# Products of constants ahead of the transposes and the decays of the first pair of heads

## The chip, the cores and the metric

The kernel runs on one core of one Trainium2 chip. The metric is the device time in microseconds (us) of one execution; less is better. A core has five engines that each work through a list of instructions of their own, in order: TensorE (PE in the profile: matrix products, and transposes as products), VectorE (DVE), ScalarE (ACT), GpSimd (POOL) and SyncE (SP, which only issues transfers here). They wait for one another through semaphores. Products land in PSUM, in banks of 128 x 512 fp32 numbers.

## The reference

One layer of a flow-matching backbone: 512 latent tokens and 256 context tokens of 1024 channels. Two mixers read the same modulated and normalised input: a bidirectional gated DeltaNet (GDN, 8 heads of 128) and an attention with low-rank keys and values. Their outputs are merged through sigmoid gates, and a squared-ReLU MLP follows. The part around the change is the GDN's input and the small matrices of its chunks:

```
qkv = silu(centred_conv(h @ w_qkv, conv_w))          # 5 taps over the tokens
q, k, v = split(qkv);  q, k = l2norm(q), l2norm(k)   # 8 heads x 128
g = -exp(a_log) * softplus(decay_logit + dt_bias);  beta = sigmoid(beta_logit)
# per head, direction and chunk of tokens:
decay = tril(exp(gc_i - gc_j))                       # gc: running sum of g
a_mat = strict_tril((beta k) k^T * decay)
t_mat = inverse(I + a_mat)                           # unit lower triangular
u, w = t_mat (beta v),  t_mat (beta k exp(gc))
qk = tril(q k^T * decay)
for each chunk: v_new = u - w S;  o = q_dec S + qk v_new;  S = S exp(g_last) + k_dec^T v_new
y = rms(o) * silu(z)                                 # z: a further projection of h
```

## The kernel before

**Products.** Activations and weights are fp32, split into a high and a low part of type fp32r (`hTh`, `hTl` for the latent input, `cTh`, `cTl` for the context, `wh`, `wl` for the weights). A product is made of three passes: high x high, high x low and low x high (`mm3`, lines 183 to 185 of before). `wchunk` loads a weight chunk (L176), casts it to `wh` on ScalarE (L177) and takes `wl` on VectorE (L178).

**PSUM.** The banks go by tags: `d` (two banks, projections), `t` (one, transposes of the inputs), `p` (two), `c` (two) and `e` (one, the decays and the products of k with k).

**A pair of heads.** The eight heads are worked on in four pairs. `gdn_in(pr)` takes, for each of the pair's two heads, K, then V, then Q: `project` (24 products of 128x512 into a `d` bank and, for K and V, 24 of 128x256 for the context into another), `convolve` (ScalarE copies the bank to `raw`, L467 and L469, and starts the sum of the five taps, L470; VectorE adds four taps, L472; ScalarE takes a tanh, L474; VectorE closes the silu, L475), and `transposes` (blocks of 128 tokens, four to a bank `t`, L488). What reads the transposes is ScalarE (for V: L522).

Between V and Q, `gdn_gram` makes the decays: for three groups of two blocks it sums running logarithms by products with a constant triangle `maskr` into bank `e` (L578), takes their exp on ScalarE (L584) into `QK` (or a buffer of its own), scales it (L589, L591), overwrites bank `e` by the products of k with k (`pk`, L596) and multiplies (`A`, L597, VectorE). ScalarE then copies the diagonal blocks of `A` to `Da` (L604) and sends them to memory (L607).

`gdn_prep(pr)` inverts the diagonal blocks: a recursion of 30 steps of two VectorE instructions each (L635, L636) on `pt`. Then ScalarE issues the transfers that put the result in its new places: `dB` (L640), `dC` (four, L643), the loads `D` from `dB` (L645) and `Q` from `dC` (L647). The chain over the chunks follows (`gdn_chain`, `gdn_out`).

**The order of the work.** The program is written as pair 0's inputs, pair 0's preparation, pair 1's inputs, a filling of six projections at low priority (`z_chunk`: a projection into a `d` bank, a tanh to `tz` on ScalarE, L880, and a VectorE instruction, L881, that reads the bank for the last time), pair 0's chain, and so on. A scheduler that runs when the program is built decides the order of each engine's list from priorities and from its own times; on the chip each list is fixed. So an added instruction can move others.

Of the kernel before, what the change touches and what calls it, by code (L numbers as in the profile page):

```python
# [18 lines left out]
KT = 8  # L19
# [58 lines left out]
def f32(ap):  # L78
    return ap.bitcast(F32)
# [3 lines left out]
def tile_layer(ctx, tc, I, out, stop=None, dbg=None):  # L83
# [4 lines left out]
    pe = nc.tensor  # L88

    def bc(ap, shape):  # L90
        return ap.to_broadcast(shape)
# [8 lines left out]
    def bank(tag):  # L100
        return ps.tile([P, 512], F32, tag=tag, name=tag, bufs=banks[tag])

    def v4(t):
        return t.rearrange("p (a b) -> p a b", b=128)
# [3 lines left out]
    hTh = hp.tile([P, KT, NL], F32R, name="hTh")  # L108
# [245 lines left out]
    maskr = cst.tile([P, 2, P], F32R, name="maskr")  # L354
# [66 lines left out]
    for b0, n in ((0, 4), (4, 2)):  # L421
        t = bank("t")[:, :128 * n]
# [18 lines left out]
    def project(chunk, with_ctx):  # L441
        pl = bank("d")
        pc = bank("d")[:, :NC] if with_ctx else None
        for k0 in (0, 4):
            for kt in range(k0, k0 + 4):
                mm3(pl, *chunk[kt], hTh[:, kt, :], hTl[:, kt, :], kt == 0, kt == KT - 1)
            if with_ctx:
                for kt in range(k0, k0 + 4):
                    mm3(pc, *chunk[kt], cTh[:, kt, :], cTl[:, kt, :], kt == 0, kt == KT - 1)
        return pl, pc  # L450
# [9 lines left out]
    def at(b):  # L460
        return 128 * b + (GAP if b >= 2 else 0)
# [14 lines left out]
        if pc is not None:  # L476
            pool.memset(raw[:, GAP + NC:GAP + NC + GAP], 0.0)

    def transposes(src, nb, tag):

        res = []
        b = 0
        while b < nb:
            n = min(4, nb - b)
            t = bank(tag)
            for q in range(n):
                c = at(b + q) if nb == 6 else 128 * (b + q)
                pe.transpose(t[:, 128 * q:128 * q + 128], src[:, c:c + 128], ident)  # L488
            res.append((t, b, n))
            b += n  # L490
        return res

    def gdn_in(pr):
        kT = gp.tile([P, 2, NG], F32, tag="kT", name="kT", bufs=2)
        qT = gp.tile([P, 2, NL], F32, tag="qT", name="qT", bufs=2)
        kn = gp.tile([P, 2, 6, P], F32, tag="kn", name="kn", bufs=2)
        vn = gp.tile([P, 2, 6, P], F32, tag="vn", name="vn", bufs=2)
        ssq = gp.tile([P, 2, 6], F32, tag="ssq", name="ssq", bufs=2)
        ssk = gp.tile([P, 2, 6], F32, tag="ssk", name="ssk", bufs=2)
        nk = gp.tile([P, 2, 6], F32, tag="nk", name="nk", bufs=2)  # L500
        r2 = gp.tile([P, 2, 6], F32, tag="r2", name="r2", bufs=2)
        junk = gx.tile([P, P], F32, tag="junk", name="junk")
        for h in range(2):
            hd = 2 * pr + h
            pl, pc = project(wchunk(I["w_qkv"][8 + hd]), True)
            convolve(pl, pc, 8 + hd, kT[:, h, :])
            for t, b, n in transposes(kT[:, h, :], 6, "t"):
                act.copy(kn[:, h, b:b + n, :], v4(t)[:, :n, :])
                for q in range(n):
                    act.activation(junk, kn[:, h, b + q, :], AF.Square, accum_out=ssk[:, h, b + q:b + q + 1])  # L510
            dve.tensor_scalar(ssk[:, h, :], ssk[:, h, :], EPS, None, op0=ALU.add)
            power(nk[:, h, :], ssk[:, h, :], 6, True)
            dve.reciprocal(r2[:, h, :], ssk[:, h, :])
        res = (kT, qT, kn, vn, ssq, ssk, nk, r2)
        for h in range(2):
            hd = 2 * pr + h
            vT = gx.tile([P, NG], F32, tag="vT", name="vT")
            pl, pc = project(wchunk(I["w_qkv"][16 + hd]), True)
            convolve(pl, pc, 16 + hd, vT)
            for t, b, n in transposes(vT, 6, "t"):  # L520
                for q in range(n):
                    act.activation(vn[:, h, b + q, :], t[:, 128 * q:128 * q + 128], AF.Copy,  # L522
                                   scale=nk[:, h, b + q:b + q + 1])
        gram = gdn_gram(pr, res)
        for h in range(2):
            hd = 2 * pr + h
            pl, _ = project(wchunk(I["w_qkv"][hd]), False)
            convolve(pl, None, hd, qT[:, h, :])
            for t, b, n in transposes(qT[:, h, :], 4, "t"):
                for q in range(n):  # L530
                    act.activation(junk, t[:, 128 * q:128 * q + 128], AF.Square,
                                   accum_out=ssq[:, h, b + q:b + q + 1])
        return res, gram
# [14 lines left out]
    def gdn_gram(pr, ops):  # L548
        kT, qT, kn, vn, ssq, ssk, nk, r2 = ops
# [13 lines left out]
        QK = gp.tile([P, 8, P], F32, tag="QK", name="QK", bufs=2)  # L563
        for b2 in range(3):
            pg = bank("e")
            for bb in range(2):
                b = 2 * b2 + bb
                rr = []
                for d in range(2):
                    for src in (ghi, glo):  # L570
                        t = gx.tile([P, 2, P], F32R, tag=f"rh{len(rr)}", name="rh")
                        sgn = 1 if d == 0 else -1
                        pool.affine_select(t, bc(f32(src[:, b, 8 * d + h0:8 * d + h0 + 2]).unsqueeze(2), [P, 2, P]),
                                           pattern=[[0, 2], [sgn, P]], compare_op=ALU.is_ge, fill=0.0, base=0,
                                           channel_multiplier=-sgn)
                        rr.append(t)
                for q in range(4):
                    pe.matmul(pg[:, 256 * bb:256 * bb + 256], maskr[:, q // 2, :],  # L578
                              rr[q].rearrange("p a b -> p (a b)"), start=(q == 0), stop=(q == 3))
            if b2 == 0:  # L580
                gam = gx.tile([P, 4, P], F32, tag="Bt", name="gam", bufs=2)
            else:
                gam = QK[:, 4 * b2 - 4:4 * b2, :]
            act.activation(gam, v4(pg), AF.Exp)  # L584
            Bt = gx.tile([P, 4, P], F32, tag="Bt", name="Bt", bufs=2)
            for bb in range(2):
                for h in range(2):
                    b = 2 * b2 + bb
                    act.activation(Bt[:, 2 * bb + h, :], f32(maskr[:, 1, :]), AF.Identity,  # L589
                                   scale=sA[:, b, 0, h:h + 1], bias=sA[:, b, 1, h:h + 1])  # L590
            dve.tensor_tensor(Bt, Bt, gam, ALU.mult)  # L591
            pk = bank("e")
            for bb in range(2):
                for h in range(2):
                    s = kT[:, h, at(2 * b2 + bb):at(2 * b2 + bb) + 128]
                    pe.matmul(v4(pk)[:, 2 * bb + h, :], s, s, start=True, stop=True)  # L596
            dve.tensor_tensor(A[:, 4 * b2:4 * b2 + 4, :], v4(pk), Bt, ALU.mult)  # L597
# [796 lines left out]
```

## Time and profile before

| | |
|---|---|
| three runs | 1318.79, 1320.42, 1323.58 us; median 1320.42 |
| profiled execution | 1319.97 us, of which the span of the trace is 1318.2 |
| PE / DVE / ACT / POOL busy | 95% / 65% / 49% / 20% of the span |
| mean granted clock of TensorE | 0.984 of 2.4 GHz |

The busy share is an average over stages with different limits. The clock that TensorE is granted has two levels, 1.2 and 2.4 GHz; in a view of a stretch 0.50 is the lower one all through it and 1.00 the upper one. In a timeline, the brackets at the end of a row hold the idle time of the engine ahead of the row and what ended it.

### The profile page before, as it was taken

What the parts mean: (1) busy time and instruction counts of PE and PEld (TensorE: products, weight loads), DVE (VectorE), ACT (ScalarE), POOL (GpSimd) and SP (SyncE); (2) the same over time, 40 slices, a digit from 0 to 9 for tenths busy, and PEclk for the clock granted to TensorE, in tenths of its full rate; (3) what the DMA queues carried; (4) which work ended last, traced back from release to release, by engine and by line L of the source; (5) the groups of instructions that cost most, each with busy time, mean ns of one, the idle gap of its engine ahead of it and who ended that gap; (6) DMA issues with size and microseconds to landing.
All of it is one profiled execution on the core that took longest, in us unless ns stands there. A gap on an engine that the chain in (4) does not pass through costs nothing. (4 is left out here: it accounts for less than half of the span.)

```text
span 1318.2 us, 21055 instructions
## 1 busy us (share of the span) xinstructions
PE 1249.4 (95%) x7406; PEld 1090.4 (83%) x7406; DVE 855.9 (65%) x1853; ACT 651.1 (49%) x1670; POOL 262.6 (20%) x369
## 2 busy tenths in 40 slices
PE   5899997988999899999989999999999999999998
PEld 4797876877889788889989998888997888888887
DVE  4655798777788768848678788676885333333332
ACT  4557574546753765366566676223453242242331
POOL 0022424314421431122100011232032010010110
PEclk9999998999999899999999999999999999999999
DMA  9332214440334114542111114766452232322232
GB/s 359 112 114 71 71 56 102 130 96 2 97 105 128 48 65 120 141 146 91 35 49 42 40 45 157 265 213 250 167 183 92 96 100 95 98 97 96 97 111 89
DMA packets 112168, 147.39 MB, mean 112 GB/s; under 512 B 45328, under 2 KB 54592, under 8 KB 111936
## 3 DMA queue, kind: packets, MB, share of 16 engines
q1 hardware_dynamic: 69728, 130.31, 29.8%
q10 hardware_dynamic: 42336, 15.76, 5.0%
q8 instruction: 58, 0.95, 0.3%
q14 instruction: 46, 0.38, 0.1%
HBM read 128.83 MB, written 17.20 MB: 111 GB/s over the span
## 5 line engine op out<-in xcount | busy, mean ns | idle before, releaser
L177 ACT CAST wh<-wf 128x512 fp32r<-128x512 f32 (+2 forms) x292 | 177.2, 610 | 358.5 <-PE d L184 288.4
L178 DVE TENSOR_TENSOR wl<-wf,wh 128x512 fp32r<-128x512 f32 (+2 forms) x268 | 183.4, 688 | 173.1 <-ACT wh L177 166.6
L183 PE MATMUL d<-hTh,wh 128*128 128x512 f32 x384 | 158.6, 413 | 5.8 <-DVE tz L881 3.5
L184 PE MATMUL d<-hTl,wh 128*128 128x512 f32 x384 | 155.6, 406 | 0.0
L185 PE MATMUL d<-hTh,wl 128*128 128x512 f32 x384 | 154.9, 403 | 0.0
L183 PE MATMUL d<-ah,wh 128*128 128x512 f32 x256 | 100.2, 393 | 0.0
L185 PE MATMUL d<-ah,wl 128*128 128x512 f32 x256 | 100.0, 393 | 0.0
L184 PE MATMUL d<-al,wh 128*128 128x512 f32 x256 | 99.3, 390 | 0.0
L183 PEld LDWEIGHTS d<-hTh,wh 128*128 128x128 f32 x384 | 74.7, 195 | 21.4 <-DVE tz L881 3.9
L1252 POOL TENSOR_TENSOR a<-r 128x512 f32<-128x512 f32 (+1 forms) x36 | 37.2, 1034 | 266.9 <-ACT r L1250 260.8
L185 PE MATMUL d<-h2h,wl 128*128 128x512 f32 x224 | 87.5, 390 | 1.7 <-DVE wl L178 1.7
L183 PE MATMUL d<-h2h,wh 128*128 128x512 f32 x224 | 87.3, 390 | 0.0
L184 PE MATMUL d<-h2l,wh 128*128 128x512 f32 x224 | 87.2, 389 | 0.0
L185 PEld LDWEIGHTS d<-hTh,wl 128*128 128x128 f32 x384 | 74.4, 194 | 15.3 <-issue 0.4
L184 PEld LDWEIGHTS d<-hTl,wh 128*128 128x128 f32 x384 | 74.8, 195 | 13.4
L1291 DVE SCALAR_TENSOR_TENSOR x<-d,mcol,x 128x512 f32<-128x512 f32 x32 | 24.0, 751 | 59.6 <-PE d L185 59.6
L178 POOL TENSOR_TENSOR wl<-wf,wh 128x512 fp32r<-128x512 f32 x24 | 35.4, 1476 | 130.7 <-ACT wh L177 130.7
L185 PEld LDWEIGHTS d<-ah,wl 128*128 128x128 f32 x256 | 48.1, 188 | 10.8
L184 PEld LDWEIGHTS d<-al,wh 128*128 128x128 f32 x256 | 48.1, 188 | 10.8
L183 PEld LDWEIGHTS d<-ah,wh 128*128 128x128 f32 x256 | 48.1, 188 | 9.8
L185 PEld LDWEIGHTS d<-h2h,wl 128*128 128x128 f32 x224 | 42.1, 188 | 10.9 <-DVE wl L178 2.1
L184 PEld LDWEIGHTS d<-h2l,wh 128*128 128x128 f32 x224 | 42.1, 188 | 8.8
(540 smaller groups left out, 3385.2 us busy)
## 6 DMA issues: line engine op xcount, KB each, us to landing
wf<-in_w_mi SPq DMA_DIRECT2D x64, 256.0 KB
wf<-in_w_mo SPq DMA_DIRECT2D x64, 256.0 KB
wf<-in_w_qkv SPq DMA_DIRECT2D x48, 256.0 KB
wm<-in_w_mod SPq DMA_DIRECT2D x40, 256.0 KB
wm<-in_w_mod SPq DMA_DIRECT2D x16, 512.0 KB
wf<-in_w_gate SPq DMA_DIRECT2D x32, 256.0 KB
wms<-in_w_mod SPq DMA_DIRECT2D x12, 512.0 KB
wf<-in_w_z SPq DMA_DIRECT2D x16, 256.0 KB
```

The source lines that it names most:

```text
L177: act.copy(wh, wf)
L178: eng.tensor_tensor(wl, wf, f32(wh), ALU.subtract)
L183: pe.matmul(po, lh, rh, start=first, stop=False)
L184: pe.matmul(po, lh, rl, start=False, stop=False)
L185: pe.matmul(po, ll, rh, start=False, stop=last)
L1252: pool.tensor_tensor(a_, r, r, ALU.mult)
L1291: dve.scalar_tensor_tensor(x1[:, ot, :], po, mcol[:, 5, ot, 0:1], x1[:, ot, :], ALU.mult, ALU.add)
```

## The change

A helper `keep_busy(t, n)` issues n products of 128x128 by 128x512, of the constant triangle `maskr[:, 1, :]` with a tile of the latent input `hTh`, into a PSUM bank that the next products overwrite from the start. For pair 0 alone, six of them stand ahead of the first bank of each of the six sets of transposes (K, V and Q of two heads), and four ahead of each of the three banks of decays: 48 products. Nothing reads what they leave.

```diff
+    def keep_busy(t, n):
+
+        for i in range(n):
+            pe.matmul(t, maskr[:, 1, :], hTh[:, i % KT, :], start=True, stop=True, skip_group_check=True)
+
-    def transposes(src, nb, tag):
+    def transposes(src, nb, tag, extra=0):
...
             t = bank(tag)
+            keep_busy(t, extra if b == 0 else 0)
             for q in range(n):
...
-            for t, b, n in transposes(kT[:, h, :], 6, "t"):
+            for t, b, n in transposes(kT[:, h, :], 6, "t", 6 if pr == 0 else 0):
...
-            for t, b, n in transposes(vT, 6, "t"):
+            for t, b, n in transposes(vT, 6, "t", 6 if pr == 0 else 0):
...
-            for t, b, n in transposes(qT[:, h, :], 4, "t"):
+            for t, b, n in transposes(qT[:, h, :], 4, "t", 6 if pr == 0 else 0):
...
             pg = bank("e")
+            keep_busy(pg, 4 if pr == 0 else 0)
             for bb in range(2):
```

In the changed program the new products have line 482, and lines behind it are 6 or 7 higher than in before (transposes L494, decays L585, exp L591, `pk` L603, transfers L647 to L654, `Da` L611, `tz` L887).

The scheduler puts the 48 products at these places of PE's list: the first four of the decays during K's projections, K's twelve during K's and V's, V's first six in the projection of V's second head, the next four decays' and V's second six during Q's, the last four decays' behind `pk`, and Q's twelve directly ahead of Q's transposes, which stand among pair 1's K projections. The lists of all engines are alike from about 295 us of before to the end.

PE, the end of the projection of V's second head (context part, 128x256) of pair 0, with the transposes of V's first head behind it. In before:

```order
L183 MATMUL d<-cTh,wh 128x256
L184 MATMUL d<-cTl,wh 128x256
L185 MATMUL d<-cTh,wl 128x256
L488 MATMUL t<-mk,vT 128x128 x4
L183 MATMUL d<-hTh,wh 128x512
L184 MATMUL d<-hTl,wh 128x512
L185 MATMUL d<-hTh,wl 128x512
```

And in the change:

```order
L183 MATMUL d<-cTh,wh 128x256
L184 MATMUL d<-cTl,wh 128x256
L482 MATMUL t<-hTh,maskr 128x512 x6
L185 MATMUL d<-cTh,wl 128x256
L183 MATMUL d<-cTh,wh 128x256
L184 MATMUL d<-cTl,wh 128x256
L185 MATMUL d<-cTh,wl 128x256
L494 MATMUL t<-mk,vT 128x128 x4
L183 MATMUL d<-hTh,wh 128x512
L184 MATMUL d<-hTl,wh 128x512
```

The six products stand four products ahead of the transposes, within the projection.

PE, the last group of pair 0's decays, during Q's projections (`pk` is `e<-kT`). In before:

```order
L185 MATMUL d<-hTh,wl 128x512
L183 MATMUL d<-hTh,wh 128x512
L184 MATMUL d<-hTl,wh 128x512
L185 MATMUL d<-hTh,wl 128x512
L596 MATMUL e<-kT 128x128 x4
L578 MATMUL e<-rh,maskr 128x256 x5
L488 MATMUL t<-mk,vT 128x128 x4
```

And in the change:

```order
L585 MATMUL e<-rh,maskr 128x256
L482 MATMUL t<-hTh,maskr 128x512 x6
L184 MATMUL d<-hTl,wh 128x512
L185 MATMUL d<-hTh,wl 128x512
L183 MATMUL d<-hTh,wh 128x512
L184 MATMUL d<-hTl,wh 128x512
L185 MATMUL d<-hTh,wl 128x512
L603 MATMUL e<-kT 128x128 x4
L482 MATMUL e<-hTh,maskr 128x512 x4
L585 MATMUL e<-rh,maskr 128x256 x4
L494 MATMUL t<-mk,vT 128x128 x4
```

Four new products stand between `pk` and the decays that take its bank; the six ahead of the transposes of V's second head have gone further up.

ACT, around the transfers that end pair 0's recursion, during pair 1's inputs and the first filling (`D_…` are the loads from `dB`). In before:

```order
L474 ACTIVATE raw<-qT 128x512
L584 ACTIVATE QK<-e 128x512
L467 COPY raw<-d 128x512
L522 ACTIVATE vn<-t,nk 128x128 x2
L470 ACTIVATE qT<-raw,convh 128x512
L177 CAST wh<-wf 128x512
L640 DMA dB<-pt 96x1024
L643 DMA dC<-pt 24x32x32 x4
L645 DMA D_1800<-dB 128x12x32
L645 DMA D_1799<-dB 128x12x32
L604 COPY Da<-A 32x384 x4
L880 ACTIVATE tz<-d 128x512
```

And in the change:

```order
L650 DMA dC<-pt 24x32x32 x4
L652 DMA D_1848<-dB 128x12x32
L652 DMA D_1847<-dB 128x12x32
L474 ACTIVATE raw<-qT 128x512
L177 CAST wh<-wf 128x512
L591 ACTIVATE QK<-e 128x512
L654 DMA Q<-dC 128x768
L467 COPY raw<-d 128x512
L528 ACTIVATE vn<-t,nk 128x128 x2
L177 CAST wh<-wf 128x512
L470 ACTIVATE qT<-raw,convh 128x512
L887 ACTIVATE tz<-d 128x512
```

The transfers stand ahead of qT's tanh, a cast and the exp into `QK`, where they stood behind them; `tz` comes ahead of `Da` (which follows the last row shown).

## Rows read from the trace of the kernel before

**Rows 1.** The page: busy time of the engines; granted clock by slices.

```profile
PE 1249.4 (95%) x7406; PEld 1090.4 (83%) x7406; DVE 855.9 (65%) x1853; ACT 651.1 (49%) x1670; POOL 262.6 (20%) x369
...
PEclk9999998999999899999999999999999999999999
```

**Rows 2.** Busy us by stretch (from:to, length, engines, clock, DMA share, GB/s).

```profile
66.00:121.00 55.00, 54.71 (x333) 49.71 (x332) 31.99 (x64) 32.39 (x94) 17.50 (x32) 1.00 0.35 100
124.60:128.00 3.40, 3.36 (x8) 2.68 (x9) 0.94 (x2) 3.40 (x11) 0.00 (x0) 0.51 0.04 15
128.00:165.60 37.60, 35.07 (x209) 30.42 (x208) 25.76 (x37) 20.24 (x51) 15.61 (x26) 1.00 0.25 64
165.00:222.00 57.00, 51.32 (x256) 42.54 (x255) 52.39 (x112) 33.76 (x85) 21.58 (x29) 0.91 0.22 63
169.00:172.30 3.30, 3.30 (x10) 2.56 (x9) 3.10 (x8) 2.61 (x10) 1.59 (x5) 0.50 0.48 155
206.00:213.30 7.30, 5.96 (x19) 5.02 (x20) 7.16 (x17) 3.29 (x7) 4.69 (x10) 0.53 0.00 0
224.40:228.00 3.60, 0.12 (x1) 0.00 (x0) 1.65 (x4) 3.52 (x9) 0.00 (x0) 0.85 0.92 138
228.00:233.40 5.40, 5.38 (x13) 4.23 (x14) 5.03 (x10) 2.05 (x9) 0.00 (x0) 0.50 1.06 263
233.40:285.00 51.60, 50.23 (x337) 43.67 (x335) 38.56 (x98) 23.14 (x52) 11.78 (x21) 1.00 0.41 110
```

The engines' columns are PE, PEld (weight loads), DVE, ACT and POOL.

**Rows 3.** PE's timeline (start, duration): V's first head, and projections behind it.

```profile
123.63 0.66 PE L488 MATMUL t<-mk,vT 128*128 128x128 f32 x4 [2.34 <-DVE vT L475]
124.64 0.80 PE L183 MATMUL d<-hTh,wh 128*128 128x512 f32 x1 [0.36 <-ACT raw L467]
...
125.66 0.63 PE L185 MATMUL d<-hTh,wl 128*128 128x512 f32 x1
126.09 0.63 PE L183 MATMUL d<-hTh,wh 128*128 128x512 f32 x1
...
129.71 0.39 PE L183 MATMUL d<-hTh,wh 128*128 128x512 f32 x1
129.94 0.39 PE L184 MATMUL d<-hTl,wh 128*128 128x512 f32 x1
```

**Rows 4.** PE's timeline: the last decay bank, Q, and K of pair 1.

```profile
140.87 0.71 PE L578 MATMUL e<-rh,maskr 128*128 128x256 f32 x4 [1.38 <-DVE A L597]
...
154.74 0.50 PE L183 MATMUL d<-hTh,wh 128*128 128x512 f32 x1 [0.79 <-ACT raw L469]
...
167.42 0.66 PE L488 MATMUL t<-mk,kT 128*128 128x128 f32 x4 [1.85 <-DVE kT L475]
```

**Rows 5.** PE's timeline: pair 1's decays, its last pk, and the filling.

```profile
207.24 1.19 PE L578 MATMUL e<-rh,maskr 128*128 128x256 f32 x4 [1.88 <-DVE A L597]
...
217.51 1.05 PE L596 MATMUL e<-kT 128*128 128x128 f32 x8
218.32 0.48 PE L183 MATMUL d<-hTh,wh 128*128 128x512 f32 x1
...
228.02 0.80 PE L183 MATMUL d<-hTh,wh 128*128 128x512 f32 x1 [3.50 <-DVE tz L881]
```

**Rows 6.** ScalarE's timeline and its queue (ACTq: DMA issues), 215 to 227 us.

```profile
215.63 0.60 ACT L584 ACTIVATE QK<-e 128x512 f32<-128x512 f32 x1
...
217.54 0.32 ACTq L640 DMA_DIRECT2D dB<-pt  x1
...
221.73 2.48 ACTq L645 DMA_DIRECT2D D<-dB  x2
224.25 2.07 ACT L604 COPY Da<-A 32x384 f32<-32x384 f32 x4 [5.57 <-issue]
...
226.34 0.60 ACT L880 ACTIVATE tz<-d 128x512 f32<-128x512 f32 x1
```

**Rows 7.** VectorE's timeline: the last step of pair 0's recursion.

```profile
217.04 0.38 DVE L636 TENSOR_TENSOR pt<-pt,tu 96x30 f32<-96x30 f32 x1
```

## The prediction

> **What bounds the kernel now.** The page comes first: TensorE (PE) is busy for 1249.4 of 1318.2 us, 95%, VectorE (DVE) for 65%, and the line of granted clocks is below its 9 in four of 40 slices [rows 1]. So nearly everything added to PE's list must be paid for, unless it stands in a hole of PE or undoes a slow clock, and the question is what the holes near the 48 new products are worth.
>
> The table of busy time by stretch follows the program from the first pair's projections to where the two programs' orders become one again (about 290 us of before). Read the PE column against the length, then the clock. From 66 to 121 us PE is busy for 54.71 of 55.00 us at clock 1.00: no hole. There the four products of the first decay bank stand, and the twelve of the first pair's two K heads. Four short stretches later show a clock of about 0.5, which is the lower of the two levels, 1.2 instead of 2.4 GHz: 124.6 to 128, 169 to 172.3, 206 to 213.3 and 228 to 233.4 us. VectorE is busy for 52.39 of the 57.00 us from 165 to 222, so in that stage it, not PE, is the limit. From 233.4 to 285 PE is busy for 50.23 of 51.60: what is late at 233 stays late [rows 2].
>
> PE's timeline then says what stands ahead of each slow stretch. At 123.63 the transposes of V's first head had waited 2.34 us for VectorE's last step of vT, and PE waited 0.36 us more before the next product: the slow stretch begins behind them [rows 3]. At 167.42 a wait of 1.85 us for kT of pair 1 precedes the second one [rows 4]. Pair 1's waits, 1.88 us at 207.24 and 3.50 us at 228.02, stand in the third stretch and ahead of the fourth [rows 5].
>
> **What the products cost.** Each is a matmul of 128x128 by 128x512 with fp32r operands, as the projections' are. In a stream at full clock those start at 129.71 and 129.94, 0.23 us apart [rows 3]; in the half-clock stream 125.66 and 126.09 are 0.43 apart. So 48 x 0.23 = **+11.0 us**; all are taken at full clock. The stationary operand is one and the same, and PE's weight loads, busy for 49.71 of 55.00 us, run beside the matmuls [rows 2], so no more is added for them. The data were in SBUF long before; no DMA, no ScalarE or VectorE instruction is added.
>
> The Trainium skill (TensorE: Matmul & The Clock Gate, section Back-to-back issue gap) gives a sustained spacing of about 131 ns for products of 512 columns. By it, the 48 would cost an estimated 6.3 us, and the forecast would be 1319.2. The row with 0.23 decides, and this trace shows no such spacing.
>
> **What they give back, place by place.**
>
> V's first head. The order shows the six products inside the end of the next head's projection, ahead of the transposes. PE comes to these transposes later by all 22 products that then stand ahead (4 + 6 + 6 + 6), 22 x 0.23 = 5.06 us. vT can be late by at most the 16 products that stand ahead of V's first convolution, 3.68 us. The difference, 1.38 us, comes off the wait of 2.34 at the least; all of it goes if VectorE has room [rows 3]. I take the middle, **-1.9**; bounds -1.4 and, with the 0.36 behind it, -2.7.
>
> The clock behind it. With the wait gone, the 3.40 us at clock 0.51 [rows 2] would take half: **-1.7**; bound 0, since a short wait may be left.
>
> The first pair's last decay bank, at 140.87. The decays wait 1.38 us there for A, VectorE's product with the previous block's pk, which frees the bank [rows 4]. The order puts the four new products behind pk, in the same bank: they wait as the decays did, and stand in no hole. **0**; bounds 0 and -1.4 (A may come earlier against PE's later list). The wait of 0.79 at 154.74 for raw [rows 4] has no new product close to it: 0, at best -0.8.
>
> kT of pair 1, at 167.42. Q's two heads put 12 products into pair 1's K projections, 2.8 us, more than the wait of 1.85 [rows 4]. The wait goes, and with it the half clock of 169 to 172.3, where PE is busy throughout [rows 2]: 1.85 + 3.30 / 2 = **-3.5**. Bound 0: VectorE is 92% busy from 165 on, and its own work may be the later one.
>
> Up to 173 us: 11.0 - 1.9 - 1.7 - 3.5 = **+3.9 us**. With every bound against the change it is +9.6 (only the 1.4 given back), with every one for it 11.0 - 2.7 - 1.7 - 1.4 - 0.8 - 3.5 = +0.9.
>
> From 173 to 290 us there are no products, but the order changes. In before, VectorE ends pair 0's recursion at 217.42 [rows 7], and ScalarE (ACT) issues seven DMAs from 217.54 to 224.21; its Da copies follow at 224.25, tz at 226.34 [rows 6], and VectorE's step on tz, which frees a d bank, ends PE's 3.50 us wait at 228.02 [rows 5]. In the order of the change the same DMAs stand ahead of qT's tanh, a weight cast and the exp that PE's next pk and the fill product's projection need, while tz now stands ahead of the Da copies. So the old stall goes and a new one can come earlier. Also VectorE takes the recursion's steps earlier against pair 1's convolutions, which moves the DMAs earlier. I take **0** for the two together; the rivals give the ends, -9.2 and +5.0.
>
> **The sum.** 1319.97 (the profiled execution, 0.45 below the median of the three runs) + 3.9 = **1323.9 us**, +0.3%. For this kernel 0.5%, 6.6 us, is about what can be told from no change: below 1313.8 is faster and above 1327.0 slower.
>
> **Rivals.**
>
> *Nothing is given back.* The products stand where PE was busy anyway, as the twelve of the K heads do, and the waits and slow stretches stay, because what PE waits for is late by as much. For it: in 66 to 121 us there is no hole, and the V and K chains depend on PE's own earlier products. Against: at V's first head the arithmetic of 22 against 16 leaves at least 1.4 us. 1319.97 + 11.0 = 1331.0 us.
>
> *A new stall at ScalarE's DMA issues; slower.* If pair 0's recursion ends no earlier than in before, the exp of pair 1's last block stands behind the issues: 224.25 + three ACT instructions of 0.60 (tanh, cast, exp) [rows 6] = 226.05, then pk, 0.81 from 217.51 to 218.32 [rows 5], and the fill's projection starts at 226.9 instead of 218.32, 8.5 late. The old 3.5 is not met again: +5.0, and 1323.9 + 5.0 = 1328.9 us. It costs nothing once the recursion ends 6.7 us ahead of where PE wants the exp (the length of the issues); a lag of 3.9 on PE's side alone covers a bit over half. Against it: the recursion's steps stand earlier in VectorE's order.
>
> *Both later stalls vanish; faster.* With PE 4 us later in its list and the recursion earlier, VectorE's backlog of 165 to 222 us is what PE was waiting for; PE then meets neither stall. 206 to 213.3 gives half of 5.96 busy at half clock, 3.0; the wait of 3.50; half of the 5.38 busy us of 228 to 233.4, 2.7 [rows 2, 5]: -9.2, 1314.7 us, and down to 1311.7 if the first part is at its best. For it: TensorE runs at full clock in every stretch of the table with no wait ahead of it. Against: VectorE's 7.16 of 7.30 us in the third stretch, which more TensorE clock does not shorten. The Trainium skill (TensorE: Matmul & The Clock Gate, section Why this matters for your kernels) advises against idle gaps between bursts of products, since the clock falls behind them. These stretches agree (0.50 to 0.53 around the waits of 1.85 to 3.50 us); by that rule alone, this rival's time would come out.
>
> **How the numbers follow.** The forecast 0.53, nothing given back 0.10, the new stall 0.20, both stalls gone 0.17. The range reaches from near the last one's best, 1312, to the first one's 1331; the forecast's own is 1320.9 (first part at its best) to 1329.6 (at its worst), mostly 1321 to 1327. Faster: 0.11, from the third rival's lower part. Slower: 0.10 + 0.15 of the second + 0.02 of the forecast's = 0.27. Same: 0.62.
>
> **What would show it.** Groups of the new products with starts 0.23 us apart (right), or 0.43 (the cost is twice as high where they stand). No wait over 1 us ahead of the transposes of V's first head, and clock 1.00 from 124 to about 173 us (right). A wait for A of about 1.4 us ahead of the new products in the last decay bank (right). A wait of PE at pair 1's last pk for the exp, with ScalarE's DMA issues just ahead of it, says that the second rival holds and by how much. The same instruction of both programs near 290 us should be 3 to 5 us later in the change, and the distance from there to the end unchanged; if that distance changes, the time came from a place that this argument leaves out. The prediction is wrong if the wait at V's first head stays above 1.4 us, or if the stretch from 173 to 290 us moves by more than 4 us either way.

## The result, and the profile after

The changed kernel takes 1326.08 us (median of 7 runs, 1324.25 to 1327.49), before 1319.2 us in the same comparison (7 runs, 1313.88 to 1323.58): ratio 1.0052, 95% interval 1.0029 to 1.0075. So it is slower by half a per cent. The forecast was 1323.9 us with a range of 1312 to 1331. The profiled execution of the change took 1324.59 us, 4.6 more than that of before, where 3.9 were forecast. The sum was nearly met; its terms were not, and they erred in both directions.

The first look is at the page of the change, engines and granted clock, as in [rows 1]:

```profile
PE 1256.5 (95%) x7454; PEld 1098.5 (83%) x7454; DVE 857.9 (65%) x1853; ACT 649.0 (49%) x1670; POOL 260.7 (20%) x369
...
PEclk9999998989999899998999999999999999999999
```

PE has its 48 instructions more and 7.1 us more of busy time. The clock is below its 9 in four of the 40 slices; before has two, which are among the four. The products themselves, in the view of their source line:

```profile
L482 PE MATMUL t<-hTh,maskr x36: 388/392/397, 92.3 to 162.8; 128*128 128x512 f32 x36
L482 PE MATMUL e<-hTh,maskr x12: 388/394/505, 69.3 to 142.9; 128*128 128x512 f32 x12
```

They last 0.39 us, as any product at full clock in [rows 3], and stand between 69 and 163 us. In PE's timeline the first six of K stand as one row, 1.53 us from the first start to the last end: (1.53 - 0.39) / 5 = 0.23 us apart, as forecast:

```profile
92.30 1.53 PE L482 MATMUL t<-hTh,maskr 128*128 128x512 f32 x6
```

Six products with one and the same stationary operand are not closer than 0.23 us here. The Trainium skill (TensorE: Matmul & The Clock Gate, section Back-to-back issue gap) has some 131 ns for a sustained stream; the measurement decides, as the prediction had it.

Next, the busy time by stretch (length, then PE, PEld, DVE, ACT, POOL, clock, DMA share, GB/s), to be held against [rows 2]:

```profile
120.00:130.00 10.00, 10.00 (x58) 8.71 (x58) 5.04 (x12) 9.29 (x26) 1.44 (x2) 1.00 0.16 53
165.00:222.00 57.00, 49.45 (x259) 41.63 (x257) 48.91 (x108) 31.72 (x82) 17.46 (x27) 0.94 0.26 66
207.40:214.20 6.80, 5.47 (x21) 4.81 (x22) 6.09 (x13) 3.26 (x7) 3.27 (x10) 0.50 0.06 21
222.00:240.00 18.00, 17.76 (x103) 14.45 (x104) 15.77 (x28) 13.06 (x32) 5.13 (x8) 1.00 0.74 202
282.00:300.00 18.00, 12.89 (x76) 12.08 (x76) 13.71 (x35) 8.55 (x25) 3.85 (x8) 0.81 0.26 67
```

From 120 to 130 us PE is busy throughout, at the full clock: the hole and the slow stretch of before are gone. So are the slow stretches at 169 and at 228. The one at 207 to 214 has stayed. The last row is new to this account: from 282 to 300 us PE is idle for 5.1 of 18 us, at a mean clock of 0.81. In before the same stretch reads:

```profile
282.00:300.00 18.00, 13.50 (x93) 12.35 (x92) 14.47 (x41) 10.06 (x28) 4.99 (x10) 0.91 0.38 84
```

PE's timeline of the change names the waits, as [rows 3 to 5] did for before:

```profile
125.19 0.60 PE L494 MATMUL t<-mk,vT 128*128 128x128 f32 x4
...
142.09 1.21 PE L482 MATMUL e<-hTh,maskr 128*128 128x512 f32 x4 [0.91 <-DVE A L604]
...
181.31 0.66 PE L494 MATMUL t<-mk,kT 128*128 128x128 f32 x4 [1.68 <-DVE kT L475]
...
222.18 1.16 PE L603 MATMUL e<-kT 128*128 128x128 f32 x8 [2.22 <-ACT QK L591]
...
282.69 2.08 PE L818 MATMUL c<-y,kn 128*128 128x128 f32 x8 [3.35 <-ACT y L805]
...
292.35 0.49 PE L837 MATMUL e<-y,Qm 128*128 128x128 f32 x2 [3.75 <-ACT y L810]
```

There is no wait ahead of the transposes of V's first head. The wait for kT has gone from the first to the second K head of pair 1. The wait for the exp at pair 1's last `pk`, which the second rival named, is there with 2.22 us. And two waits of 3.35 and 3.75 us, for `y`, stand in pair 0's chain over the chunks, in a stage that the prediction had only counted as "PE is busy".

What each place did to the end is best seen by matching the two traces: the n-th matmul of a line in one with the n-th in the other, and the difference of their starts. Executions of this program differ by up to 4.5 us in when the first projections begin (loads at the start), so the difference at 60 us of before is taken off. "End" is the last product. All runs told below are in the table; minus is earlier than before.

```
us after before, at us of before:      119    130    173    273    300    end   median (ratio)
the change                             2.5   -0.8    0.8   -2.7    2.8    4.5   1326.08 (1.0052)
e1_k_only       12 long, K             1.8   -1.6   -2.8   -2.8   -2.8   -4.3   1316.06 (0.9986)
e2_v0_only      6 long, V's first      0.0   -1.4   -3.4  -10.2   -1.1   -3.2   1317.86 (0.9995)
e3_late_issues  change, DVE slower     2.5   -0.8    0.8   -3.2    3.1    7.7   1327.26 (1.0071)
e4_early_issues before, issues early   0.0   -0.1   -0.1    0.0    1.0    4.0   1326.79 (1.0068)
e5_v0_taps      before, DVE order      0.0   -0.3    0.7   -4.8    2.3    0.1   1321.97 (1.0021)
e6_k_short      12 short, K            0.2   -2.9   -2.6   -5.2    2.2    2.1   1322.13 (1.0020)
e7_sync_issues  change, SyncE issues   2.5   -0.8    0.8   -3.4   -2.1    2.2   1323.06 (1.0021)
e8_sync_before  before, SyncE issues   0.0   -0.1   -2.2   -3.6   -2.1    3.6   1325.02 (1.0051)
e9_all_short    48 short               0.6   -3.2   -3.2   -7.3   -1.5    3.8   1326.27 (1.0068)
e10_k_double    24 long, K             4.0    0.9   -0.9   -2.4    3.3    3.5   1325.49 (1.0043)
e11_k_short_sync 12 short, SyncE       0.2   -2.9   -2.9   -5.2    2.4    7.7   1324.78 (1.0044)
```

The change is 0.8 us late at 173 us, where the sum had 3.9; it is 2.7 us *early* at 273 us; and it loses 5.5 us from 273 to 300. From 300 us to the end 1.7 more are lost, while the lists of all engines are the same there; what differs in that part is where the clock is low (at 317, around 443 and 593 us in the change; around 438, 589 and 647 in before). The difference between the two moves mostly at these places: by +1.4 us around 440, +1.5 around 590 and -1.7 around 647.

### The profile page after: what moved, and what is told of

Its sections match the earlier page's. It is cut to its first block, busy times and chain, and to the rows that moved or that the text cites. A ratio compares the mean times of both kernels' runs of the same rounds, so it can differ in the third digit from the quotient of the medians.

```text
span 1322.9 us, 21150 instructions
## 1 busy us (share of the span) xinstructions
PE 1256.5 (95%) x7454; PEld 1098.5 (83%) x7454; DVE 857.9 (65%) x1853; ACT 649.0 (49%) x1670; POOL 260.7 (20%) x369
## 5 line engine op out<-in xcount | busy, mean ns | idle before, releaser
L178 DVE TENSOR_TENSOR wl<-wf,wh 128x512 fp32r<-128x512 f32 (+2 forms) x268 | 183.1, 687 | 177.3 <-ACT wh L177 167.8
L183 PE MATMUL d<-hTh,wh 128*128 128x512 f32 x384 | 155.3, 404 | 0.7 <-ACT raw L467 0.6
L184 PE MATMUL d<-hTl,wh 128*128 128x512 f32 x384 | 152.7, 398 | 0.0
L178 POOL TENSOR_TENSOR wl<-wf,wh 128x512 fp32r<-128x512 f32 x24 | 35.3, 1471 | 131.3 <-ACT wh L177 131.3
```

The lines of the kernel that those rows point to most:

```text
L178: eng.tensor_tensor(wl, wf, f32(wh), ALU.subtract)
L183: pe.matmul(po, lh, rh, start=first, stop=False)
L184: pe.matmul(po, lh, rl, start=False, stop=False)
```

## The experiments

The first theory after the result: the products pay for themselves, by holes and by clock, up to 273 us; the loss comes from ScalarE's list at pair 0's chain, where the change puts the DMA issues and copies of pair 1 ahead of `y`. The rival: the 48 products are the loss, at 0.23 us each.

**K's products alone** (`e1_k_only`), and **those of V's first head alone** (`e2_v0_only`):

```diff
-            for t, b, n in transposes(vT, 6, "t", 6 if pr == 0 else 0):
+            for t, b, n in transposes(vT, 6, "t", (0, 0)[h] if pr == 0 else 0):
...
-            for t, b, n in transposes(qT[:, h, :], 4, "t", 6 if pr == 0 else 0):
+            for t, b, n in transposes(qT[:, h, :], 4, "t", (0, 0)[h] if pr == 0 else 0):
...
-            keep_busy(pg, 4 if pr == 0 else 0)
+            keep_busy(pg, (0, 0, 0)[b2] if pr == 0 else 0)
```

This is the first one; the second has `(0, 0)` at K and `(6, 0)` at V instead.

> Only the twelve products of the first pair's two K heads, where PE is busy for 54.71 of 55.00 us. ScalarE's list at pair 1's transfers and pair 0's chain reads as in before. If products cost their spacing where there is no hole, the same instruction of both programs is 12 x 0.23 = 2.8 us later just ahead of V's first transposes, the wait there stays near 2.3 us, and 2.8 us are left at 273 us of before and at the end: 1322.0 against 1319.2. If even there half comes back, as in the changed kernel's trace (16 products left 2.7 of 3.7), it is about 2 us. The rival, that the loss comes from ScalarE's order alone, says under 1 us.

> Only the six products ahead of the transposes of V's first head, where PE waits for 2.34 us and has the lower clock for 3.4 us behind. If a hole pays for its products: 1.4 us of products lie in the wait, the transposes come no later than in before, and with the clock at 1.00 behind them the same instruction is 1.5 to 2 us earlier at 129 us of before (0 if the clock falls all the same, since a wait of 1 us is left). Further on the order changes a little; about 1317.5 against 1319.2 at the end if it holds, 1319 to 1320.6 if the clock is not kept.

Measured: with K's twelve alone 0.9986 of before (0.9971 to 1.0001; 12 runs against 23), with V's six alone 0.9995 (0.9979 to 1.0010). K's products were expected to be pure cost, and the kernel is, if anything, a little faster with them. They cost 1.8 us at 119 us of before, yet at 130 us the program is 1.6 us early: V's first transposes do not wait, although none of their own products is there.

```profile
122.70 0.60 PE L494 MATMUL t<-mk,vT 128*128 128x128 f32 x4
124.38 0.50 PE L183 MATMUL d<-hTh,wh 128*128 128x512 f32 x1 [1.08 <-ACT raw L467]
```

That is PE's timeline of the run with K's products. vT was ready at 122.7 us instead of 123.6 (both from the same start), with PE later ahead of it. So here the wait did not go because products stood in it: vT was finished earlier. Two lists have a part in that. VectorE's timeline in before, at the four taps (L472) of V's first head:

```profile
115.73 2.08 DVE L472 SCALAR_TENSOR_TENSOR vT<-raw,convh,vT 128x770 f32<-128x770 f32 x2 [3.12 <-ACT vT L470]
118.61 0.17 DVE L511 TENSOR_SCALAR ssk<-ssk 128x6 f32<-128x6 f32 x1 [0.80 <-ACT junk L510]
118.69 1.02 DVE L472 SCALAR_TENSOR_TENSOR vT<-raw,convh,vT 128x770 f32<-128x770 f32 x1
119.62 0.18 DVE L513 RECIPROCAL r<-ssk 128x6 f32<-128x6 f32 x1
119.72 0.65 DVE L178 TENSOR_TENSOR wl<-wf,wh 128x512 fp32r<-128x512 f32 x1
120.29 1.02 DVE L472 SCALAR_TENSOR_TENSOR vT<-raw,convh,vT 128x770 f32<-128x770 f32 x1
```

And in the change:

```profile
116.48 4.19 DVE L472 SCALAR_TENSOR_TENSOR vT<-raw,convh,vT 128x770 f32<-128x770 f32 x4 [0.91 <-ACT vT L470]
```

In before K's normalisation stands between the second and the third tap in VectorE's list, and waits for ScalarE's sums (0.80 us idle); a weight part stands ahead of the last tap. In the change, and with K's products alone, the scheduler has put all four taps first. They take 4.19 us in one go, against 5.6 from the first start to the last end.

The larger part is ScalarE's, which starts vT's sum (L470) ahead of the taps. In before L470 stands behind eight instructions for the squares of K (L510):

```profile
112.26 0.38 ACT L469 COPY raw<-d 128x256 f32<-128x256 f32 x1
...
113.16 0.31 ACT L510 ACTIVATE junk<-kn 128x128 f32<-128x128 f32 x1
...
114.78 0.93 ACT L470 ACTIVATE vT<-raw,convh 128x770 f32<-128x770 f32 x1
```

And with K's products alone, ahead of them, as in the change:

```profile
113.61 0.37 ACT L469 COPY raw<-d 128x256 f32<-128x256 f32 x1
...
114.35 0.95 ACT L470 ACTIVATE vT<-raw,convh 128x770 f32<-128x770 f32 x1
```

From the last copy of raw (L469) to L470 it is 2.52 us in before and 0.74 in this run and in the change, 1.8 less. From L470 to the end of vT it is 8.79 and 8.17 us (8.15 in the change), 0.6 less, although the taps save 1.4: VectorE's last step also waits for ScalarE's tanh.

The run with V's six alone shows the other way. There L470 stands behind the squares and the taps in three parts, as in before, and PE's timeline (3.4 us later from its start on) has

```profile
126.58 0.66 PE L494 MATMUL t<-mk,vT 128*128 128x128 f32 x4 [0.56 <-DVE vT L475]
```

The wait is 0.56 us instead of 2.34. Of the 1.78 less, 1.38 is the time of the six products (6 x 0.23), and 0.40 comes from vT, which ends that much earlier. The clock stays full behind it, and at 130 us the program is 1.4 us early, where 1.5 to 2 were expected. Here products do stand in a wait, and the clock that they keep up pays.

**Two tests of that.** One moves the normalisation behind the taps without any product (`e5_v0_taps`): a small VectorE instruction that reads vT after its fourth tap is put ahead of it. The other keeps K's twelve products, at 64 columns (`e6_k_short`).

```diff
         act.activation(dst, raw[:, o + 2:o + 2 + n], AF.Identity, scale=convh[:, ch, 2:3])
         for i in (0, 1, 3, 4):
             dve.scalar_tensor_tensor(dst, raw[:, o + i:o + i + n], convh[:, ch, i:i + 1], dst, ALU.mult, ALU.add)
+        if then is not None:
+            then(1, dst)
...
-            pe.matmul(t, maskr[:, 1, :], hTh[:, i % KT, :], start=True, stop=True, skip_group_check=True)
+            pe.matmul(t[:, 0:64], maskr[:, 1, :], hTh[:, i % KT, 0:64], start=True, stop=True, skip_group_check=True)
```

> The kernel before, without any product; the normalisation of K's second head is made to wait for the four taps of V's first head on VectorE, which then run nearly in one go, as they do in the change and in the run with K's products alone. If the time given back at V's first head comes from VectorE's order: the wait of 2.34 us falls to 1 us or less, and the same instruction is 1.3 us earlier at 130 us of before with the clock falling as before, about 3 us with the clock kept. If it takes the products: wait above 2 us, no difference at 130 us. The end of the program is open, since the later order changes too: 1314 to 1322.

> K's twelve products with 64 columns instead of 512: nearly no time on PE, VectorE's order at V's first head as with the long ones. If the products' own time is the cost there and the order the gain: 2 us earlier than with the long ones at 119 us of before, and V's first transposes no later than with the long ones (122.7 us), the wait ahead of them coming back as 1 to 2 us; at 130 us the same or up to 1.7 us later if the clock falls behind that wait. If the products' filling is the gain, the wait is back at 2.3 us and at 130 us the program stands where before did.

Measured, `e5_v0_taps`: the edit did not reach its aim. The scheduler put a weight part (L178), which itself waits for a cast, ahead of the fourth tap, and ScalarE's L470 stands behind the squares of K as in before. The fourth tap comes 0.6 us earlier, and vT at 123.6 us as in before, with the wait of 2.33 us and the slow clock behind it. So this run does not test the order that the change has. `e6_k_short` has the four taps in one go:

```profile
117.33 4.20 DVE L472 SCALAR_TENSOR_TENSOR vT<-raw,convh,vT 128x770 f32<-128x770 f32 x4 [0.91 <-ACT vT L470]
```

and PE's timeline has, at V's first transposes:

```profile
124.78 0.66 PE L494 MATMUL t<-mk,vT 128*128 128x128 f32 x4
126.59 0.50 PE L183 MATMUL d<-hTh,wh 128*128 128x512 f32 x1 [1.16 <-ACT raw L467]
```

(This execution began 3.3 us later than before's.) The short products cost 0.2 us up to 119 us, and at 130 us the program is 2.9 us early. The wait is gone with hardly any time in the products; that it would come back as 1 to 2 us, as expected, did not happen. vT ends 2.2 us earlier than in before, from the same start: 1.7 of them stand already at its first tap, by ScalarE's order, and 0.5 come behind it. So what is given back here comes from the order of ScalarE, and less of VectorE, and the clock with it. No run changes ScalarE's list alone.

In the change both ways act. PE's products make L469 2.3 us later than in before. An estimate from these rows: with before's 11.3 us from L469 to the end of vT, vT would be ready at 125.9 us, and PE, which comes to the transposes at 125.0, would wait 0.9 us instead of 2.34; with the 8.9 us of the change's order it is ready at 123.5. By this, the products take some 1.4 us of the wait and the order the rest.

In the eleven runs and the change, the clock is low behind V's first transposes in the three that keep the wait of 2.33 us (`e4`, `e5`, `e8`), as in before, and in none of the nine others. The product time itself is the cost: twelve long products instead of twelve short ones, with the lists otherwise nearly the same up to 200 us, take away 1.3 us of that gain.

**The price of a product with the order held** (`e10_k_double`): 24 long ones ahead of K's transposes; the lists of the other engines read, but for a few rows, like those of `e6_k_short`. And **all 48 as short ones** (`e9_all_short`).

```diff
-            for t, b, n in transposes(kT[:, h, :], 6, "t", 6 if pr == 0 else 0):
+            for t, b, n in transposes(kT[:, h, :], 6, "t", (12, 12)[h] if pr == 0 else 0):
```

(V's, Q's and the decays' have none in the first; the second has the change's counts, with the 64 columns shown above.)

> 24 long products ahead of K's transposes instead of 12 short ones; the lists of all engines read like those of the run with the short ones but for the products' places. It prices a product with the order held: 24 x 0.23 - 12 x 0.03 = 5.2 us later than with the short ones just ahead of V's first transposes; if VectorE's work sets the pace from 165 to 222 us and at the chain, most of it is gone by 300 us (0 to 2 us left). If PE sets it, 4 to 5 us are left at 300 us and at the end.

> All 48 products at the change's places, but with 64 columns. VectorE's order at V's first head is the change's. If products cost their own time wherever no wait takes them (theory), the same instruction is 3 to 6 us earlier than in the change at 173 us of before, where the change is 0.8 later than before (from the same start). If the products fill waits for nothing, it stands within 1 us of the change there. At the chain of pair 0 ScalarE's order is between before's and the change's (both y behind the transfers of dC, ahead of the loads D), so there 2 to 4 us may be lost as well.

Measured: against `e6_k_short`, the 24 long ones are 3.8 us later at 119 us and at 130, 1.7 at 173, 2.8 at 273, 1.1 at 300. The short ones were dearer than the 0.03 us put down for them: six stand in 0.75 us, some 0.1 each. So the expected difference is 24 x 0.23 - 12 x 0.1 = 4.3, and PE pays almost all of it while it is the bound. Of 3.8 us, 1.1 are left at 300 us: PE's lag is taken by the waits of the stages where VectorE and the chain set the pace. All 48 as short ones are 4.0 us earlier than the change at 173 us and 4.3 at 300. So the products' time is paid, at about 4 of the some 6 us (48 x 0.13) that long ones take more than short ones (the lists of the two also differ in places, so this is no clean price). The kernel with the short ones is no faster at the end for all that (1.0068, 1.0044 to 1.0092): it loses 5.8 us between 273 and 300 us, and 5.3 from there to the end.

**ScalarE's issues at the chain.** Four runs bear on the 5.5 us of 273 to 300. ScalarE's timeline and its queue there, in the change:

```profile
274.92 0.33 ACTq L647 DMA_DIRECT2D dB<-pt  x1
275.28 4.61 ACTq L650 DMA_DIRECT2D dC<-pt  x4
279.99 1.67 ACTq L652 DMA_DIRECT2D D<-dB  x2
281.75 0.62 ACT L177 CAST wh<-wf 128x512 fp32r<-128x512 f32 x1 [12.01 <-DMA dC<-pt]
282.27 0.36 ACT L805 ACTIVATE y<-c,bkd 128x128 f32<-128x128 f32 x1
...
288.53 2.07 ACT L674 COPY A<-D 32x384 f32<-32x384 f32 x4 [5.12 <-DVE D L670]
290.62 1.03 ACT L704 COPY Sx<-Q 32x384 f32<-32x384 f32 x2
291.67 0.37 ACT L805 ACTIVATE y<-c,bkd 128x128 f32<-128x128 f32 x1
291.94 0.62 ACT L810 ACTIVATE y<-c,br 128x128 f32<-128x128 f32 x2
```

And in before:

```profile
277.67 0.37 ACT L798 ACTIVATE y<-c,bkd 128x128 f32<-128x128 f32 x1 [5.66 <-DVE y L797]
277.84 0.34 ACTq L640 DMA_DIRECT2D dB<-pt  x1
278.20 0.42 ACTq L643 DMA_DIRECT2D dC<-pt  x1
278.73 0.37 ACT L798 ACTIVATE y<-c,bkd 128x128 f32<-128x128 f32 x1 [0.69 <-POOL Em L752]
278.74 3.31 ACTq L643 DMA_DIRECT2D dC<-pt  x3
...
287.39 0.37 ACT L798 ACTIVATE y<-c,bkd 128x128 f32<-128x128 f32 x1 [2.65 <-DVE y L797]
...
290.52 2.06 ACT L667 COPY A<-D 32x384 f32<-32x384 f32 x4
```

In before both `y` of the step come ahead of most of pair 1's issues, and the next step's ahead of the copies. In the change they stand behind all seven, and the next step's behind the six copies of pair 1's preparation and its wait of 5.12 us for VectorE. PE's two waits for `y` (3.35 and 3.75 us) end with them. The engine takes its list in order; the Trainium skill says so of ScalarE and VectorE too (Perfetto Trace Analysis, section Tensor Engine Instruction), and these rows agree: `y` starts 0.5 us after the start of the cast ahead of it, which itself started when the last issue was through.

`e3_late_issues` makes pair 1's recursion end 2.6 us later, by three more VectorE instructions, so that the scheduler puts the issues behind `y` again; `e4_early_issues` raises the priority of the issues in before:

```diff
+        if pr == 1:
+            for i in range(3):
+                dve.tensor_scalar(flat(pt), flat(pt), 1.0, None, op0=ALU.mult)
         pool.memset(flat(pt)[:, 0:1024:33], 1.0)
...
-        act.dma_start(dB.rearrange("c q (d a) b -> (c q d) (a b)", d=4), flat(pt))
+        with tc.high_priority(offset=300 if pr == 1 else 0):
+            act.dma_start(dB.rearrange("c q (d a) b -> (c q d) (a b)", d=4), flat(pt))
```

(in the second, the issues of dC and D likewise; each diff is against its own kernel).

> The changed kernel with three more instructions on VectorE at the end of pair 1's recursion (a product by 1.0 over all of pt, about 1.1 us each), which put ScalarE's transfers of pair 1 behind the y of pair 0's chain, as in before. Theory (order): the waits of 3.35 us at 282.69 and 3.75 us at 292.35 of the change shrink to before's 2 and 0.7, and at 300 us of before the program is 1 us earlier to 0.5 later than before instead of 3.0 later; at the end about 1321 against the change's 1326. Rival (the products themselves are the loss): the three instructions on the busy VectorE make it no faster, 1326 to 1329.

> The kernel before, without any product, with a higher priority for pair 1's transfers behind its recursion: one of the two y of pair 0's second chain step goes behind all seven issues, as both do in the change. Theory (order): PE gets a wait of about 3 to 4 us near 283 us that before has not, up to 4 us later at 300 us, 1321 to 1323 at the end. Rival (products): no change, 1319 to 1320.

Measured: `e3_late_issues` 1.0071 (1.0049 to 1.0093), no faster than the change. The wait at 282 us is gone, but pair 1's preparation then stands ahead of the next steps (the first of them waits behind a weight cast that ScalarE starts only after the issues), with waits of PE of 2.95, 1.75 and 1.94 us, and 6.3 us are lost from 273 to 300 instead of 5.5: the stall has only moved. `e4_early_issues` has one of the two `y` behind the issues, a wait of 1.53 us for it, and 1.0 us lost at 300 us. That is the direction of the theory with about half the wait and a quarter of the loss expected. (Its end, 4.0 late, comes from after 300 us, where its lists differ as well.)

`e7_sync_issues` and `e8_sync_before` let SyncE issue pair 1's transfers, in the change and in before; `e11_k_short_sync` does so with the twelve short products:

```diff
-            act.dma_start(t, dB[:, q].rearrange("c p b -> p c b"))
+            (nc.sync if pr == 1 else act).dma_start(t, dB[:, q].rearrange("c p b -> p c b"))
```

(and the same at dB, dC and Q).

> The changed kernel with pair 1's eight transfers behind the recursion issued by SyncE, not by ScalarE. Theory (ScalarE's issues ahead of the y): the wait of 3.35 us at 282.69 goes, and at 300 us of before it is 2 to 4 us earlier than the change (3.0 later than before); the end 1322 to 1324. Rival (products, or VectorE's order): waits stay, 1326. If only the copies of pair 1's preparation on ScalarE remain ahead of the later y, the second wait (3.75 us) stays and half of it comes back.

> The same transfers on SyncE in the kernel before, without products: there one y stands ahead of the issues and one among them. Theory: 0 to 1 us earlier at 300 us, 1318 to 1319.5 at the end; it tells what the move to SyncE is worth by itself, to set the run above against.

> The twelve short products of K with pair 1's transfers issued by SyncE. With the short ones alone, 7 us were lost between 280 and 300 us of before, with waits of 3.58 and 2.59 for y. Theory: without ScalarE's issues those waits go down by half or more, and at 300 us the program is 1.5 to 3 us earlier than before (from the same start), 1315 to 1318 at the end. Rival (the waits come from VectorE's order): 5 us lost again, 1322.

Measured: in the change, with SyncE issuing, 1.3 us are lost from 273 to 300 instead of 5.5, and 1.0021 of before (1.0002 to 1.0040) is left of 1.0052. PE's timeline there:

```profile
280.27 0.71 PE L818 MATMUL c<-y,kn 128*128 128x128 f32 x4 [0.45 <-ACT y L805]
284.12 0.49 PE L834 MATMUL p<-s,qT 128*128 128x128 f32 x2 [2.24 <-DVE s L826]
```

The wait for `y` is 0.45 instead of 3.35 us. PE's list is the change's up to about 330 us, so this compares well. But ScalarE's list has not only lost the issues: of the next step's `y`, one now stands ahead of the six copies and one between them, and VectorE's list differs a little too. So ScalarE's list, issues and copies together, was about 4 us of the change's loss up to 300 us; the share of the issues alone is not shown. By itself the move gains nothing: before with it loses 1.5 us from 273 to 300, where 0 to 1 us earlier was expected. (That it is slower at the end, 1.0051, 1.0034 to 1.0068, comes from after 300 us, where its lists differ up to 630 us.) And with the short products it did not help at all: 7.6 us lost from 273 to 300, as against 7.4 without the move. There the stall stands on VectorE:

```profile
288.23 0.58 DVE L667 STREAM_TRANSPOSE T<-D 128x384 f32<-128x384 f32 x1 [3.78 <-DMA D<-dB]
288.73 0.56 DVE L826 SCALAR_TENSOR_TENSOR s<-s,egl,c 128x128 f32<-128x128 f32 x2
```

The first is pair 1's: it waits 3.78 us for the loads from dB, and pair 0's new state `s`, which PE waits for (3.72 us), stands behind it; with the short products alone the same instruction waits 4.62 us. So it is not the issues as such. Whatever of pair 1's preparation stands in an in-order list ahead of pair 0's chain hands its own wait to the chain: the issues on ScalarE in one program, the first reader of the loads on VectorE in another.

## Why the prediction came out as it did

*The price of a product*, 0.23 us at full clock: right, by the row of six and by the run with 24. That the first sixteen (K's twelve and four decays') are paid in full: measured 2.5 us at 119 us of 3.7, so a third came back in a stretch that had been called free of holes. K's twelve alone leave 1.8 of 2.8 there. The traces show where: up to 100 us every product is paid, and 1.0 us comes back at one place. In before the product L272 stands at 101.76 us between `pk` (101.27) and the next projection (102.24); in the change, and with K's products alone, it stands elsewhere, and the projection starts 0.15 us behind the first start of `pk` instead of 0.97. It is PE's own order that gains there. The busy share did not show this hole, since the rows overlap, but the starts do. Why L272 starts late in before was not tried.

*V's first head*: the sum had -1.9 and -1.7, with -2.7 and -1.7 as the best case, and the wait and the slow clock did go. From 2.5 at 119 us to -0.8 at 130, in spite of six products, 4.7 us were given back: the best case and 0.3 more. The arithmetic of 22 against 16 products was sound as a bound (the run with V's six alone and the estimate above bear it out), but it took the order of ScalarE and VectorE at this place as given: vT was not late by up to 3.7 us but ended 0.1 us earlier than in before. The order shown ahead of the prediction had PE's list here, and not those of the engines that make vT.

*The last decay bank*: the four products wait behind `pk` for A, as forecast, 0.91 instead of 1.38 us. A new wait of 1.20 us for qT at 158 us was in no term.

*kT of pair 1*: the wait of 1.85 us and the slow clock behind it went, as forecast, but half of it came back: 1.68 us at the second head. Up to 173 us the sum was 3.9 and the measurement 0.8, within the bounds given (0.9 to 9.6) but for 0.1.

*From 173 to 290 us, taken as 0*: this term was two large ones that nearly cancel. The second rival's mechanism came at its place, with 2.22 us instead of 8.5, since pair 0's recursion ended at 214.7 instead of 217.4; the stall at the filling and the slow stretch behind it went, as the third rival had it, though that at 207 to 214 us stayed. This gave 3.5 us back from 173 to 273. Then pair 0's chain lost 5.5, by the second rival's mechanism at a place that it had not looked at: pair 1's issues and copies instead of pair 0's issues. The table of stretches ended at 285 us with PE busy for 50.23 of 51.60, and "what is late at 233 stays late" was read from it; what is *early* at 273 did not stay early. So the term of 0 was wrong in its two parts, and that the total came near the forecast is luck: it is owed to this cancellation. The same holds for the signs that the prediction set itself: at 290 us the change is 4.0 us later than before (3 to 5 forecast) and 4.5 at the end, and from 173 to 290 it moves by some 3 us (4 were allowed), but on the way it is 2.7 us early.

*A misreading*: the page's line of clocks [rows 1] is below its 9 in two of 40 slices, not in four. No term rests on it.

*What is open.* From 300 us to the end the change loses 1.7 us in the profiled pair, and the other runs between -2.1 and 5.8. The change has before's lists there, and its larger steps stand where the clock is low; these stretches differ from run to run. Each of the eleven runs has lists that differ from before's behind 320 us as well (up to 343 us in `e2`, 480 in `e1`, 550 in `e7`, 600 to 660 in the others), so their ends and medians do not price the places ahead. Which part of the 6.9 us between the medians belongs to this was not settled. Each place after 120 us was also read from one execution of each kernel: `e8_sync_before`, whose lists read as before's up to there, is 2.2 us early at 173 us because the clock did not fall at 169. `e1` and `e2`, with before's lists from about 131 to 200 us, gain 1.2 and 2.0 us between 130 and 173 in the same way. So the clock's part of what the change gives back at kT may be the execution's and not the change's.

## What to carry to other kernels

An instruction that a scheduler must place is paid three times: its own time, here close to its row wherever the engine has no hole; the order of the engine that it waits for; and the order of every stage behind it. Where the lists differ, compare those of the engine that each wait names, and of the engines ahead of it, up to the place where the programs become one again, and price the first instruction of a later stage that stands ahead of an earlier stage's chain. Only K's twelve products, with lists of all engines that read as before's from about 130 to 320 us, kept what they had gained (-2.8 us at 173, 273 and 300); every other program that was early at 273 us lost between 1.3 and 9.1 us by 300.

## What had not been expected of the hardware

Six products of 64 columns with one stationary operand took 0.75 us, some 0.1 each, against 0.23 for 512 columns: an eighth of the columns is not an eighth of the time. And PE waits of 1.08 and 1.16 us in front of a projection (K's long and short products) were followed by the full clock, where the 2.34 and 0.36 us of before were followed by half of it, up to 128 us; the four executions with a wait of 2.33 or 2.34 us there have it, and the nine without have not. At pair 1's first kT the length of the wait does not tell them apart: behind 1.85 us (before) and 2.31 us (`e6_k_short`) the clock fell, behind 2.16 us (`e1_k_only`) it did not.
